# TensorE in program order: a delta rule and an attention woven between steps of twelve products

## The chip, the cores and the metric

The kernel runs on one core of one Trainium2 chip. The metric is the device time in microseconds of one execution; the time given for a kernel is the median of its runs. The profile and the trace are of one more execution, taken by the hardware profiler.

## The reference

One inference step of a two-layer decoder on 256 prompt tokens and 8 x 4 sample tokens (288 columns in all), model width 2048. Cut to what matters:

```python
for l in range(2):
    h = rmsnorm(x, norm_mix[l])
    if l == 0:   # gated delta rule, 12 heads of 128, chunks
        qkv, z, a, b, q_mem = split(h @ w_in)            # 2048 -> 4608 + 1536 + 24 + 512
        qkv = silu(causal_conv4(qkv)); q, k = l2norm(q), l2norm(k)
        beta, g = sigmoid(b), -exp(a_log) * softplus(a + dt_bias)
        # per chunk: solve (I + strict(k k^T * decay) * beta) [u, w] = [v beta, k beta gamma]
        # u -= w S; o = q_g S + (q k^T * decay) u; S = S * g_end + k_end^T u
        y_tok = rmsnorm(o) * silu(z)
    else:        # four causal pooling windows, a grouped projection
        y_tok, q_mem = pool_mixer(h)
    y_mem = cross_attn(q_mem, mem_k[l], mem_v[l])        # 4 heads, 256 memory tokens
    x = x + concat(y_tok, y_mem) @ w_out[l]
    x = x + (silu(rmsnorm(x) @ w_gate) * (rmsnorm(x) @ w_up)) @ w_down
y = rmsnorm(x)
```

Memory keys and values of the prompt are projected in the kernel (`mem_kv`); those of the eight samples are read from a cache (16 loads of 512 KB for each layer). States and caches are outputs too.

## The kernel before

Activations lie transposed, 128 features by 288 tokens to a tile. Every large product is computed from three products of rounded parts: a weight tile is split into `whi` (by ScalarE, L130) and `wlo` (by VectorE, L131), an activation into `xh` and `xl`, and L160, L161 and L162 issue `wh*xh`, `wh*xl` and `wl*xh`, 288 columns each. A weight chunk is one load of 512 KB (three buffers, tag `wraw`), and gives eight such products, 24 matmuls. `gemm_steps` is a generator over chunks: it yields once for a chunk. `mem_kv` does the same with 512 columns (L286 to L288). Products accumulate in four PSUM banks (`acc`); everything else that TensorE does writes one of four `aux` banks.

The order of the stages: `kq(0)` projects keys and queries of the first two heads while x is loaded; `x_norm` loads the rows of x (L248) for the norm's scale `rs0`; `alpha_beta` and `rates`, then `decays`, make the decay rates; then six units of two heads each. `Unit.keys` builds the triangular matrices and inverts them: squares and scales, `la` (L794, L800), then four levels of 32x32 blocks (L852 transposes on VectorE, L860 multiplies, ScalarE copies, L876 multiplies, VectorE merges at L885), then joins of blocks up to 128 and `wk`. `Unit.values` follows with the values, the states and the output; its last loads and stores are the sample states (L1011, L1104 to L1123). `gate` transposes the result and multiplies it into `y`. `drain` takes one piece of each of its generators in turn: a piece of `values` of one unit, one of `keys` of the next, one of `attention(0)`, one chunk of the projections for later units. After the sixth unit come the output projection `out_proj`, the feed-forward network (`ffn`, two thirds of all products), then the second layer: queries, `mem_kv(1)`, the pooling projections with `attention(1)` between them, `out_proj`, `ffn` and the final norm.

The code is a program in one order; a scheduler at compile time then lays out each engine's own queue: it takes instructions by priority (earlier in the program first, weights' splits raised by `high_priority`) when its own model of time says that they are ready. On the chip each engine, and SP's queue of loads, runs its list as laid out, and waits by semaphores. So in the kernel before a small matmul can stand anywhere in TensorE's queue, and a product of the next chunk can be put ahead of a part that the model thinks late.

`Norm.rstd` is the scale of a norm that the feed-forward network and the queries need: three column sums on TensorE (L210), a reciprocal square root of some twelve small VectorE operations (L105 to L111), three matmuls that spread it over the partitions (L235).

Of the kernel before, what the change touches and what calls it, by code (L numbers as in the profile page):

```python
# [16 lines left out]
P = 128  # L17
# [35 lines left out]
def VZ(n):  # L53
    return [24 + 2 * n, 25 + 2 * n] + ([36 + 2 * n, 37 + 2 * n] if n < 5 else [])
# [3 lines left out]
def body(ctx: ExitStack, tc: tile.TileContext, i: dict, o: dict):  # L58
# [13 lines left out]
    EV = 100  # L72

# [70 lines left out]
    def gemm_steps(chunk, ncols, kt, act, on_block, ks=2, order=None, bank=None, parts=1):  # L144
# [4 lines left out]
        for k0 in order:  # L149
            nk = min(ks, kt - k0)  # L150
            w = wchunk(chunk(k0 // ks), nk, ncols, parts=parts if k0 == 0 else 1)
            last = k0 == order[-1]
            kj = [(k, j) for k in range(nk) for j in range(nb)]
            for k, j in sorted(kj, key=lambda t: t[1]) if last else kj:
# [4 lines left out]
                en = last and k == nk - 1  # L159
                nc.tensor.matmul(pv, wh, xh, start=st, stop=False)  # L160
                nc.tensor.matmul(pv, wh, xl, start=False, stop=False)  # L161
                nc.tensor.matmul(pv, wl, xh, start=False, stop=en)  # L162
                if en:
                    on_block(j, pv)
            yield
# [14 lines left out]
    class Norm:  # L180
# [25 lines left out]
        def rstd(self):  # L206
            ps = aux()
            for t in range(3):
                rows = P if t < 2 else NS
                nc.tensor.matmul(  # L210
# [19 lines left out]
    def spread_psum(r):  # L230

        ps = aux()
        for t in range(3):
            rows = P if t < 2 else NS
            nc.tensor.matmul(  # L235
# [8 lines left out]
    def row_squares(src, rows, out):  # L244

        for h in range(2):
            t = wpool.tile([P, 1024], F32, name="rows", tag="wraw", bufs=3)[:rows]
            nc.sync.dma_start(t, src[:, h * 1024 : (h + 1) * 1024])  # L248
            nc.scalar.activation(t, t, AF.Square, accum_out=out[:rows, h : h + 1])

    def mem_norm():
        q = sp.tile([P, 2, 2], F32, name="mq", tag="mq", bufs=1)
        for t in range(2):
            row_squares(i["mr"][t * P : (t + 1) * P], P, q[:, t])
# [16 lines left out]
    def mem_kv(l, mem, part_tile, half, kt_, v_):  # L271
        mt = []
        pss = [[acc() for _ in range(2)] for _ in range(2)]
        for k0 in range(0, KT, 2):
            for k in (k0, k0 + 1):
                mt.append(split(mem(k), memw(l, k), hi=part_tile(), lo=part_tile()))
            for part in range(2):
                w = wchunk(i["wkv"][l, part, k0 // 2], 2, 512)
                for t in range(2):
                    for k in range(2):  # L280
# [5 lines left out]
                        nc.tensor.matmul(pv, xh, w[k][0], start=st, stop=False)  # L286
                        nc.tensor.matmul(pv, xl, w[k][0], start=False, stop=False)
                        nc.tensor.matmul(pv, xh, w[k][1], start=False, stop=en)  # L288
                yield
        for t in range(2):  # L290
# [11 lines left out]
            for h in range(NMH):  # L302
                nc.tensor.transpose(
# [8 lines left out]
    pad = cp.tile([P, 2, NMH, 2 * SHIFT + TS], F32, name="pad")  # L312
# [26 lines left out]
    rs0 = sp.tile([P, NT], F32, name="rs0", tag="rs0", bufs=1)  # L339
# [18 lines left out]
    def attention(l, ys, g2, s4, ahead):  # L358
        y = ys[NH:]
        for h in range(NMH):  # L360
            ps = aux()
            pv = ps.rearrange("p (t m) -> p t m", t=2)
            for t in range(2):
                nc.tensor.matmul(
# [13 lines left out]
            for t in range(2):  # L378
                nc.vector.tensor_scalar(e[:, t, :], e[:, t, :], sm[:, t : t + 1], None, op0=ALU.mult)
            pt = aux()  # L380
            ptv = pt.rearrange("p (m t) -> p m t", m=2)
            for m in range(2):
                for t in range(2):
                    nc.tensor.transpose(
# [3 lines left out]
            nc.vector.tensor_copy(pT, ptv)  # L388
            po = aux()
            for m in range(2):  # L390
                nc.tensor.matmul(
# [4 lines left out]
            yield  # L396
# [1175 lines left out]
```

## Time and profile before

| what | value |
|---|---|
| three runs | 2729.25, 2724.21, 2725.95 us; median 2725.95 |
| the profiled execution | 2727.26 us, of which the trace's span is 2725.5 us |
| TensorE, matmuls and weight loads | 2657.4 us and 2571.2 us busy, 21400 of each |
| VectorE, ScalarE, GpSimd | 1593.0, 1237.9 and 316.5 us busy |
| mean granted TensorE clock | 0.987 of full speed |
| moved by DMA | 455.86 MB, mean 167 GB/s |

How to read it: matmuls are pipelined, so the time of one is longer than its distance to the next, and a busy TensorE is not one at its peak. In the rows below PE is the matmuls' record and PEld that of the weight loads, of which each matmul has one. "Idle before" names what an engine waited for. The delta rule and the first attention run up to about 650 us, the first feed-forward network up to about 1590 us, the pooling layer with the second attention from 1600 to 1800 us, the second feed-forward network up to the end.

### The profile page before, as it was taken

Reading aid. Unit: us, or ns where it says so; the run is one execution under the profiler, and the core shown is the slowest. Engines: PE = TensorE matmul, PEld = TensorE weight load, DVE = VectorE, ACT = ScalarE, POOL = GpSimd, SP = SyncE. Lnnn points to the kernel's source line nnn. Section 1 sums busy time; section 2 is a strip of 40 time slices with the busy share of each in tenths; the row PEclk is TensorE's granted clock in tenths of the full one; section 3 lists DMA queues with packets and bytes.
Section 4 is the critical chain, followed back from the end, with each engine's and each line's share of the span. In section 5 each row is a group of like instructions: output and inputs, shape, how many; then the busy total and the mean of one; then the engine's idle time right before and its main releaser. Section 6 shows DMA issues by size and latency. Waiting matters only on the chain. (4 is left out here: it accounts for less than half of the span.)

```text
span 2725.5 us, 54445 instructions
## 1 busy us (share of the span) xinstructions
PE 2657.4 (98%) x21400; PEld 2571.2 (94%) x21400; DVE 1593.0 (58%) x3178; ACT 1237.9 (45%) x2407; POOL 316.5 (12%) x620
## 2 busy tenths in 40 slices
PE   7899999999999999999999999999999999999998
PEld 6888888788999999999999988899999999999997
DVE  5558776777655555445555566766555544555544
ACT  5454444444544444344444454455444433444443
POOL 0103221221101000000010111111001000001000
PEclk8999999999999999999999999999999999999998
DMA  7374345434545445455554575655455544545453
GB/s 255 122 233 134 102 151 171 143 118 169 164 164 169 167 166 168 165 169 165 170 166 167 166 248 160 216 174 162 164 170 164 169 167 166 167 166 170 164 170 128
DMA packets 133424, 455.86 MB, mean 167 GB/s; under 512 B 19440, under 2 KB 22000, under 8 KB 133168
## 3 DMA queue, kind: packets, MB, share of 16 engines
q1 hardware_dynamic: 133168, 452.38, 50.1%
q8 instruction: 168, 2.75, 0.4%
q14 instruction: 88, 0.72, 0.1%
HBM read 439.46 MB, written 12.86 MB: 166 GB/s over the span
## 5 line engine op out<-in xcount | busy, mean ns | idle before, releaser
L131 DVE TENSOR_TENSOR wlo<-wraw,whi 128x512 fp32r<-128x512 f32 (+1 forms) x1548 | 1066.6, 696 | 976.7 <-ACT whi L130 946.7
L130 ACT CAST whi<-wraw 128x512 fp32r<-128x512 f32 (+1 forms) x1548 | 939.7, 614 | 1214.2 <-PE acc L161 1128.4
L160 PE MATMUL acc<-a,whi 128*128 128x288 f32 x4864 | 1445.0, 297 | 19.0 <-ACT whi L130 19.0
L162 PE MATMUL acc<-a,wlo 128*128 128x288 f32 x4864 | 1443.8, 297 | 0.0
L161 PE MATMUL acc<-a,whi 128*128 128x288 f32 x4864 | 1443.4, 297 | 0.0
L160 PEld LDWEIGHTS acc<-a,whi 128*128 128x128 f32 x4864 | 918.6, 189 | 24.8 <-ACT whi L130 20.2
L162 PEld LDWEIGHTS acc<-a,wlo 128*128 128x128 f32 x4864 | 918.2, 189 | 5.6 <-issue 2.4
L161 PEld LDWEIGHTS acc<-a,whi 128*128 128x128 f32 x4864 | 918.9, 189 | 3.9 <-issue 1.4
L160 PE MATMUL acc<-b,whi 128*128 128x288 f32 x960 | 282.3, 294 | 0.0
L162 PE MATMUL acc<-b,wlo 128*128 128x288 f32 x960 | 282.3, 294 | 0.0
L161 PE MATMUL acc<-b,whi 128*128 128x288 f32 x960 | 282.3, 294 | 0.0
L1227 POOL TENSOR_TENSOR b<-b,rrow 128x288 f32<-128x288 f32 x88 | 89.4, 1034 | 1259.8 <-ACT b L1226 1259.8
L160 PEld LDWEIGHTS acc<-b,whi 128*128 128x128 f32 x960 | 180.1, 188 | 0.0
L162 PEld LDWEIGHTS acc<-b,wlo 128*128 128x128 f32 x960 | 180.1, 188 | 0.0
L161 PEld LDWEIGHTS acc<-b,whi 128*128 128x128 f32 x960 | 180.1, 188 | 0.0
L195 POOL TENSOR_TENSOR ssum<-ssum,sq 128x288 f32<-128x288 f32 x56 | 53.0, 947 | 427.6 <-ACT sq L194 425.6
L286 PE MATMUL acc<-whi,a 128*128 128x512 f32 x128 | 50.9, 406 | 5.1 <-ACT a L174 5.1
L288 PE MATMUL acc<-wlo,a 128*128 128x512 f32 x128 | 50.2, 393 | 0.0
L1225 DVE TENSOR_TENSOR b<-acc,rrow 128x288 f32<-128x288 f32 x88 | 40.1, 456 | 16.1 <-PE acc L162 16.1
L1226 ACT ACTIVATE b<-b 128x288 f32<-128x288 f32 x88 | 36.6, 439 | 26.1 <-DVE b L1225 25.8
L1231 DVE TENSOR_TENSOR b<-acc,b 128x288 f32<-128x288 f32 x88 | 39.9, 454 | 1.6
L690 DVE SCALAR_TENSOR_TENSOR ckq<-xp,cols,ckq 128x312 f32<-128x312 f32 x72 | 37.2, 547 | 0.7 <-ACT ckq L688 0.5
(378 smaller groups left out, 1607.0 us busy)
## 6 DMA issues: line engine op xcount, KB each, us to landing
wraw<-in_wgu_dram SPq DMA_DIRECT2D x352, 512.0 KB, 3.3
wraw<-in_wdn_dram SPq DMA_DIRECT2D x176, 512.0 KB, 3.2
wraw<-in_w_dram SPq DMA_DIRECT2D x103, 512.0 KB, 3.7
wraw<-in_wout_dram SPq DMA_DIRECT2D x64, 512.0 KB, 3.3
wraw<-in_wkv_dram SPq DMA_DIRECT2D x32, 512.0 KB, 4.2
wraw<-in_w1u_dram SPq DMA_DIRECT2D x32, 384.0 KB, 3.2
s<-in_dS_dram SPq DMA_DIRECT2D x12, 512.0 KB, 4.8
out_dram<-s SPq DMA_DIRECT2D x12, 512.0 KB, 3.8
```

Of the source, the lines that this page charges most:

```text
L130: nc.scalar.copy(hi[:, :n], src)
L131: nc.vector.tensor_tensor(lo[:, :n], src, hi[:, :n].bitcast(F32), op=ALU.subtract)
L160: nc.tensor.matmul(pv, wh, xh, start=st, stop=False)
L161: nc.tensor.matmul(pv, wh, xl, start=False, stop=False)
L162: nc.tensor.matmul(pv, wl, xh, start=False, stop=en)
L195: nc.gpsimd.tensor_tensor(self.sum, self.sum, q, op=ALU.add)
L286: nc.tensor.matmul(pv, xh, w[k][0], start=st, stop=False)
L288: nc.tensor.matmul(pv, xh, w[k][1], start=False, stop=en)
L690: nc.vector.scalar_tensor_tensor(c[:, :312], xp[:, q : q + 312], convw(q, f), c[:, :312], op0=ALU.mult, op1=ALU.add,)
L1225: nc.vector.tensor_tensor(t, ps, rs, op=ALU.mult)
L1227: nc.gpsimd.tensor_tensor(t, t, rs, op=ALU.mult)
L1231: nc.vector.tensor_tensor(t, ps, t, op=ALU.mult)
```

## The change

All matmuls and transposes now go through `mm` and `tr`, which give each one an ordering edge to the one before it: TensorE's queue is the program's order, and the scheduler still orders the other engines. A chunk yields twice, after each twelve matmuls (a step; nine in the pooling projections, three in their grouped ones). `weave` counts steps: before each it runs those parts of its lanes that are due, and a lane's `yield n` says that its next part comes n steps later. `keys` becomes 16 parts (at steps 0, 4, 9, 10, 12, 13, 15, 16, 18, 19, 21, 22, 24, 25, 26 and 28 of a unit's weave), `values` 8 parts (from step 4: 4, 6, 8, 10, 13, 16, 18, 20, the last with what was `gate`), an attention head three. A unit's weave has 32 steps of products for units 0 to 2, 24 for units 3 and 4, and for unit 5 ten steps of the output projection, which now starts there. Rows of x and of the memory are loaded into the tag `ck` (three buffers) where they took weight buffers; `rates` and `decays` move behind the first projection, as a lane. `rstd` stays a plain call. Some copies and scalings of `keys` and `attention` go from VectorE to ScalarE, two predicated copies become one, the padded queries of the attention's value part get a buffer of their own for each of two samples, and the last state product of `values` moves up and holds an `aux` bank of its own (`pe`) beside `po` and `pz`.

```diff
+    def in_order(ins):
+
+        if last[0] is not None:
+            tc.add_manual_dep(
+                ins.ins, last[0].name,
+                mybir.DependencyInfo(
+                    mybir.DependencyClass.NoSync, mybir.DependencyReason.DATA
+                ),
+                reason="order",
+            )
+        last[0] = ins.ins
+        return ins
+
+    def mm(*args, **kw):
+        return in_order(nc.tensor.matmul(*args, **kw))
...
+            if last_:
+                kj.sort(key=lambda t: t[1])
+            n = 0
+            for k, j in kj:
...
+                n += 1
+                if n % max(1, len(kj) // 2) == 0:
+                    yield
...
-    def row_squares(src, rows, out):
+    def row_squares(src, rows, out, tile_):
 
         for h in range(2):
-            t = wpool.tile([P, 1024], F32, name="rows", tag="wraw", bufs=3)[:rows]
+            t = tile_([P, 1024])[:rows]
...
-    def mem_norm():
+    def mem_norm(tile_):
...
+                    yield
...
-    pad = cp.tile([P, 2, NMH, 2 * SHIFT + TS], F32, name="pad")
+    pad = cp.tile([P, 2, 2, NMH, 2 * SHIFT + TS], F32, name="pad")
...
-    rs0 = sp.tile([P, NT], F32, name="rs0", tag="rs0", bufs=1)
+    rs0 = sp.tile([P, NT], F32, name="rs0", tag="rrow", bufs=1)
...
-    def x_norm():
+    def x_rows(tile_):
         q = sp.tile([P, 3, 2], F32, name="xq", tag="xq", bufs=1)
         for t in range(3):
             rows = P if t < 2 else NS
-            row_squares(i["xr"][t * P : t * P + rows], rows, q[:, t])
+            row_squares(i["xr"][t * P : t * P + rows], rows, q[:, t], tile_)
+        return q
+
+    def x_norm(q):
...
-                nc.vector.tensor_scalar(e[:, t, :], e[:, t, :], sm[:, t : t + 1], None, op0=ALU.mult)
+                nc.scalar.activation(e[:, t, :], e[:, t, :], AF.Copy, scale=sm[:, t : t + 1])
+            yield 4
...
-            nc.vector.tensor_copy(pT, ptv)
+            nc.scalar.copy(pT, ptv)
+            yield 2
...
-                nc.gpsimd.tensor_copy(pad[:, :, :, SHIFT : SHIFT + TS], pT[:, :, :, b, :])
+                nc.gpsimd.tensor_copy(pad[:, b % 2, :, :, SHIFT : SHIFT + TS], pT[:, :, :, b, :])
...
+    class Lane:
+
+
+        def __init__(self, gen, wait=0):
+            self.gen, self.at, self.live = gen, wait, True
+
+        def go(self, now):
+            while self.live and self.at <= now:
+                n = next(self.gen, self)
+                if n is self:
+                    self.live = False
+                else:
+                    self.at = now + max(1, n or 1)
+
+    def weave(filler, lanes, side=None):
+
+        now, more = 0, True
+        if side:
+            side.at = 0
+        while more or any(t.live for t in lanes):
+            for t in lanes + ([side] if side else []):
+                t.go(now)
+            if more:
+                more = next(filler, lanes) is not lanes
+            now += 1
...
+    def out_proj(l, order, after, ys=None):
+
+        ys = {} if ys is None else ys
+
+        def load(g, c):
+            p = order.index(c)
+            for k in (2 * q + n for q in order[p : p + 2] for n in range(2)):
+                if k not in ys:
+                    ys[k] = split(y[k])
+            return i["wout"][l, g, c]
...
-        gp = tiles("u", 8)
+        gp = tiles("u", 4)
+        gp4 = tiles("la", 2)
...
-            rates(pab)
...
+            return pab
...
-                dt = decay(h0)
-                pk, pz, pq = aux(), aux(), aux()
+                pk, pz = aux(), aux()
+                pq = pz[:, 320:326]
...
-                nc.vector.tensor_copy(krf.rearrange("p c d -> p (c d)"), pk)
-                nc.vector.tensor_copy(kr_s.rearrange("p h d -> p (h d)"), pz[:NS3, : 2 * P])
+                nc.scalar.copy(krf.rearrange("p c d -> p (c d)"), pk)
+                nc.scalar.copy(kr_s.rearrange("p h d -> p (h d)"), pz[:NS3, : 2 * P])
...
-                yield
+                yield 4
 
                 stt = nc.vector.scalar_tensor_tensor
-                la = {}
+                la = gp4([P, 2, 2, 2, P])
+                la = {t: la[:, t] for t in range(2)} | {"all": la}
...
-                    for t in range(2):
-                        cp_(
-                            uc[bl(q), 2 * t : 2 * t + 2, :], mask(1, bl(q), 2),
-                            la[t][bl(q), :, 0, bl(q)],
-                        )
+                    cp_(
+                        uc[bl(q), 0:4, :].rearrange("p (t h) c -> p t h c", t=2),
+                        lev[1][bl(q)].unsqueeze(1).unsqueeze(1).broadcast_to([32, 2, 2, 32]),
+                        la["all"][bl(q), :, :, 0, bl(q)],
+                    )
...
+                yield 5
...
+                    yield 1
...
+                    yield 2
...
-                cc(U[lo, :, hi], pZ[lo])
+                nc.scalar.copy(U[lo, :, hi], pZ[lo])
...
+                pe = aux()
+                for hh in range(2):
+                    mm(H(pe, hh), kend[:, 1, hh, :], u[1][:, hh, :], start=True, stop=True)
...
-        x_block(0)
-        next(first)
-        for n in range(1, 6):
+        for n in range(6):
             x_block(n)
-            next(first)
+            steps(first, 2)
         load_constants()
         nc.sync.dma_start(cst[:, :, 3:27], i["convT"])
         nc.sync.dma_start(alog, i["a_log"][0].partition_broadcast(P))
         nc.sync.dma_start(dtb, i["dt_bias"][0].partition_broadcast(P))
-        x_norm()
-        steps(first, 1)
-        alpha_beta()
-        steps(first, 1)
-        decays()
+        xq = x_rows(ck)
+        ab = alpha_beta()
+        steps(first, 2)
+        x_norm(xq)
         drain(first)
 
         def mem_part():
-            mem_norm()
+            mem_norm(ck)
             yield from mem_kv(0, mem_blocks(ck), lambda: at(F32R)[:, :NM], ga, KT_, V_)
 
-        drain(units[0].keys(), chain(vz(0), project_q(), mem_part(), kq(1)))
+        z = lambda n: project(96 + 4 * n, [44 + 2 * n, 45 + 2 * n])
+
+        def rates_keys():
+            rates(ab)
+            yield 4
+            decays()
+            yield 2
+            yield from units[0].keys()
+
+        weave(chain(vz(0), project_q(), mem_part(), kq(1)), [Lane(rates_keys(), 1)])
+        att = Lane(attention(0, y, ga, ck, 2))
+        out = out_proj(0, (0, 1, 2, 3, 4, 6, 7, 5), lambda k: n1.add(k, x[k], ffnw(0, k)))
+        n1 = Norm()
+        x = []
         for n in range(6):
+            lanes = [Lane(units[n].values(), 0 if n == 5 else 4)]
             if n < 5:
-                gem = [vz(n + 1)] + ([kq(n + 2)] if n < 4 else [])
-                side = take(att, 20 if n == 4 else 4) if n >= 1 else iter(())
-                drain(units[n].values(), units[n + 1].keys(), side, chain(*gem))
-            else:
-                conv_state()
-                drain(units[n].values(), project(100, [46, 47]))
-            units[n].gate()
+                lanes.insert(0, Lane(units[n + 1].keys()))
+            if n == 4:
+                lanes.append(att)
+            filler = (
+                chain(kq(n + 2), vz(n + 1)) if n < 4 else chain(vz(5), z(0), z(1)) if n == 4
+                else take(out, 10)
+            )
+            weave(filler, lanes, att if 1 <= n < 4 else None)
+        conv_state()
...
-                    steps(gate, 6)
+                    steps(gate, 12)
...
-        n1 = Norm()
-        drain(out_proj(0, (0, 1, 2, 3, 4, 6, 7, 5), lambda k: n1.add(k, x[k], ffnw(0, k))))
+        drain(out)
...
-        drain(
+        weave(
             chain(
                 project_u(3), project_u(2), group(3, acc), project_u(1), group(2, acc),
                 project_u(0),
             ),
-            slowly(att),
+            [Lane(attention(1, y, ga, s4, 3), 3)],
```

## Rows read from the trace of the kernel before

**Rows 1.** The page, busy time of TensorE.

```profile
PE 2657.4 (98%) x21400; PEld 2571.2 (94%) x21400; DVE 1593.0 (58%) x3178; ACT 1237.9 (45%) x2407; POOL 316.5 (12%) x620
```

**Rows 2.** Windows: busy us of PE, PEld, DVE, ACT, POOL, clock; sum over 200:650.

```profile
250.00:300.00 50.00, 49.48 (x558) 45.87 (x558) 34.99 (x89) 25.40 (x53) 9.66 (x32) 1.00 0.55 169
...
sum 450.00, PE 427.42 PEld 380.12 DVE 338.87 ACT 203.55 POOL 122.16; mean PE 47.49 PEld 42.24 DVE 37.65 ACT 22.62 POOL 13.57
```

**Rows 3.** The same view, other stretches: feed-forward network, pooling layer.

```profile
1000.00:1200.00 200.00, 200.00 (x1521) 200.00 (x1521) 98.69 (x155) 80.75 (x135) 4.10 (x4) 1.00 0.50 167
1600.00:1700.00 100.00, 98.42 (x580) 86.70 (x579) 68.12 (x146) 51.40 (x110) 12.53 (x30) 1.00 0.56 179
1700.00:1800.00 100.00, 96.93 (x814) 90.07 (x814) 72.54 (x174) 49.00 (x106) 17.47 (x51) 0.98 0.63 207
```

**Rows 4.** Timeline of TensorE, two levels of the inversion: start, us, line.

```profile
105.96 0.29 PE L162 MATMUL acc<-a,wlo 128*128 128x288 f32 x1
106.18 0.45 PE L860 MATMUL aux<-h,u 32*32 32x32 f32 x32
106.56 0.40 PE L160 MATMUL acc<-a,whi 128*128 128x288 f32 x1
106.80 0.30 PE L161 MATMUL acc<-a,whi 128*128 128x288 f32 x1
...
107.15 0.45 PE L876 MATMUL aux<-uc,h 32*32 32x32 f32 x32
...
108.65 0.45 PE L860 MATMUL aux<-h,u 32*32 32x32 f32 x32
```

**Rows 5.** Timeline of TensorE: one unit's first key transposes, its first level.

```profile
393.35 0.49 PE L751 MATMUL aux<-ident,ckq 128*128 128x128 f32 x3
...
421.87 0.42 PE L860 MATMUL aux<-h,u 32*32 32x32 f32 x29 [1.45 <-ACT v L1077]
```

**Rows 6.** Timeline of TensorE, the start.

```profile
41.23 0.61 PE L160 MATMUL acc<-a,whi 128*128 128x288 f32 x1 [12.40 <-ACT whi L130]
...
49.46 4.66 PE L611 MATMUL aux<-a,wraw 128*32 128x288 f32 x64
```

**Rows 7.** Timeline of SP's queue, the start.

```profile
24.43 9.43 SPq L248 DMA_DIRECT2D rows<-in_xr_dram  x6
36.84 0.35 SPq L120 DMA_DIRECT2D wraw<-in_w_dram  x1
```

**Rows 8.** Timeline of TensorE: `rates`, `decays`.

```profile
54.82 0.53 PE L532 MATMUL aux<-masks,g 128*128 128x32 f32 x4
...
73.81 0.67 PE L576 MATMUL aux<-gg,masks 128*128 128x24 f32 x4 [1.07 <-DVE gg L558]
...
75.46 0.46 PE L576 MATMUL aux<-gx,ones 32*128 32x96 f32 x2
...
78.54 0.60 PE L594 MATMUL aux<-gam,masks 32*128 32x6 f32 x4
```

**Rows 9.** Timeline of TensorE, the first products of `mem_kv(0)`.

```profile
137.36 1.22 PE L286 MATMUL acc<-whi,a 128*128 128x512 f32 x2 [3.97 <-ACT a L174]
```

**Rows 10.** Timeline of TensorE: a norm's scale, before the first feed-forward network.

```profile
759.00 0.51 PE L210 MATMUL aux<-ones,ssum 128*128 128x1 f32 x4
759.45 0.40 PE L160 MATMUL acc<-a,whi 128*128 128x288 f32 x1
...
763.07 1.04 PE L235 MATMUL aux<-ident,c3y 128*128 128x128 f32 x6
```

**Rows 11.** Timeline of TensorE, the last norm's scale at the end.

```profile
2712.72 1.75 PE L235 MATMUL aux<-ident,c3y 128*128 128x128 f32 x6 [2.50 <-DVE c3y L111]
```

**Rows 12.** Line L457 in 1600:1800: what TensorE sat idle for, us, times.

```profile
  POOL pad L454: 6.8, 7
```

**Rows 13.** VectorE's groups by form in 200:650: count, busy us, mean ns.

```profile
L131 DVE TENSOR_TENSOR wlo<-wraw,whi 128x512 fp32r<-128x512 f32 x159 | 110.5, 706 | 58.5 <-ACT whi L130 52.5 <-PE aux L876 1.9 <-ACT u L915 1.3
...
L841 DVE COPY_PREDICATED uc<-levels,u 32x64 f32<-32x64 uint8 x40 | 14.0, 386 | 0.3
```

More of the change, by code (lines that the diff above doesn't have):

```diff
@@ L158, in gemm_steps @@
                 st = k0 == order[0] and k == 0
[L159 to L162, printed above, removed]
+                en = last_ and k == nk - 1
+                mm(pv, wh, xh, start=st, stop=False)
+                mm(pv, wh, xl, start=False, stop=False)
+                mm(pv, wl, xh, start=False, stop=en)
                 if en:
                     on_block(j, pv)
-            yield
+                n += 1
+                if n % max(1, len(kj) // 2) == 0:
+                    yield
     def split(src, scale=None, hi=None, lo=None):
@@ L476, in drain, with steps @@
     def drain(*gens):
-        live = list(gens)
-        while live:
-            for g in list(live):
-                if next(g, live) is live:
-                    live.remove(g)
+        for g in gens:
+            for _ in g:
+                pass
+    def steps(g, n):
+        for _ in range(n):
+            next(g, None)
     def take(g, n):
@@ L486, in take, with on @@
             yield
-    def steps(g, n):
-        for _ in range(n):
-            next(g, None)
+    class Lane:
[26 more added lines that the diff above has]
+            return i["wout"][l, g, c]
+        for g in range(4):
+            def on(j, ps):
+                k = 4 * g + j
+                nc.vector.tensor_tensor(x[k], x[k], ps, op=ALU.add)
+                after(k)
+            yield from gemm_steps(
+                lambda c: load(g, c), 512, KT, lambda k: ys[k], on,
+                order=[2 * c for c in order],
+            )
     y = [None] * 16
@@ L760, in keys @@
                     )
-                for hh in range(2):
-                    for t in range(3):
-                        rows = P if t < 2 else NS
-                        n = t * 2 + hh
-                        nc.tensor.matmul(
-                            pq[:rows, n : n + 1], q2[hh][:, t * P : t * P + rows], ones[:, 0:1],
-                            start=True, stop=True,
-                        )
                 ts = nc.vector.tensor_scalar
@@ L797, in keys @@
                         )
+                    for hh in range(2):
+                        ts_ = slice(t * P, (t + 1) * P)
                         n = t * 2 + hh
@@ L811, in keys @@
                     )
+                for hh in range(2):
                     for m, sc in ((0, nrb), (1, rk)):
@@ L1283, in body @@
         queries = gemm_steps(lambda c: i["w1q"][c], 512, KT, n2.act, on_q)
-        steps(queries, 6)
+        steps(queries, 12)
         rs1 = n2.rstd()
@@ L1366, in body @@
         )
-        steps(out, 5)
+        steps(out, 8)
         drain(group(1, aux))
         drain(group(0, aux))
-        steps(out, 4)
+        steps(out, 8)
         nc.sync.dma_start(o["pool"], st)
```

197 lines of the change are left out of this document (94 added, 103 removed).

## The prediction

> **What bounds the kernel now.** I read the page first, then windows by stage, then the timelines of the places that stood out. TensorE is the bound from end to end: its matmuls' record is busy 98% of the span [rows 1]. How much of that is product? In the feed-forward network 1521 matmuls take 200 us, 131.5 ns each, and both records are full [rows 3]; a step of twelve is 1.58 us. Nothing can be won there. In the delta rule the two records part: from 200 to 650 us the matmuls' record misses 22.6 of 450 us, the weight loads' 69.9 [rows 2]. Every matmul has a weight load, so a stretch in which the loads pause is one in which the array isn't fed, though a long matmul record still covers it. I take the 69.9 us as the room there. VectorE has 338.9 us of work in the same 450, ScalarE 203.6 [rows 2]: neither is full, but VectorE is near enough to hold up a chain. Other room: 12.4 us of waiting for weights at the start [rows 6], 4.0 before the memory projection [rows 9], 23.2 us of paused weight loads in the pooling layer [rows 3].
>
> [...] By the one record here the core could give 22.6 us at most, by the other 69.9; the full stretch of the feed-forward network, where the two agree, speaks for the second.
>
> **The change, part by part.** Sums are against the profiled execution, 2727.3 us (2725.5 of span and 1.8 around it), 1.3 above the median of the runs shown.
>
> *The weave, 200 to 650 us.* It adds no product. Each part that stands between products costs a turn: before the 32x32 group the distance is 0.22 us in place of 0.13, after it 0.24 in place of 0.13, so 0.20 for the two [rows 4]. With 24 parts in each of six units and 22 of the attention, 166 parts, this is 33 us that no order removes. Do the parts come in time? In a level the second group follows the first after 0.97 us and the next level after 1.50 [rows 4]; the weave gives them one and two steps, 1.6 and 3.2 us, so there is cover as long as VectorE's queue is not over 1.6 us late. The long chain is the one from the first key transposes to the first level: 28.5 us in the unit shown, with 1.45 of waiting at its end [rows 5]. The weave gives it nine steps, 14.2 us, and whatever parts stand between. It is also made shorter: half as many predicated copies, which were 40 of 386 ns [rows 13], and copies that leave VectorE; ScalarE has 246 us free for them [rows 2]. What stands against it: VectorE's splits of weights alone are 110.5 us [rows 13], and a late one now stops TensorE, where before another instruction could stand there. Units 3 and 4 have 24 steps for 28 due, and unit 5 has ten for some eighteen, so the last parts there have no cover. I cannot price every part; I take the best stretch of the kernel before, 4.13 us of pause in 50 with units running [rows 2], as what the whole core becomes: nine times this is 37.2, a gain of 32.7 us. Bounds: nothing, and 69.9 - 33.2 = 36.7.
>
> [...]
>
> *The start.* SP issues the six row loads over 9.43 us, each waiting for a weight buffer, and the next weights go out only at 36.84 [rows 7]; TensorE waits 12.4 us [rows 6]. In buffers of their own three rows go at once, and weights needn't wait behind the others if the compiler's list puts them ahead; the rows still end when they end, the spread of the norm now stands before the last chunk, and behind it everything on TensorE. So what can move into the hole is the seventh chunk (24 x 0.1315 = 3.2) and the 64 small products of `alpha_beta`, 4.66 [rows 6]: 7.8 us. Bounds: 0 (SP's list keeps the rows first, with wab's load and the weights queued behind them) and 12.4.
>
> *Rates and decays.* Before, 19.0 us pass between the products of `rates` and those of `decays`, and TensorE idles 1.07 of them [rows 8], because products of the next projection stand between. Now four steps, 6.3 us, stand there, and what is late stops all of TensorE. The chain is some forty small VectorE operations among the convolutions of four heads. Bounds: 19.0 - 6.3 = 12.7 if nothing speeds it up; the nearest row for a bare chain is a norm's root, a third of it, 3.6 us from 759.45 to 763.07 [rows 10], so 10.9 - 6.3 = 4.6. Inside `decays` the last products wait for an exponential, 2.6 us from 75.92 to 78.54 [rows 8], with no step between. I take 9 + 3 = 12 lost; bounds 4.6 + 2.6 = 7.2 and 12.7 + 2.6 = 15.3.
>
> *Memory projection.* The squares of the memory's rows leave the weight buffers as well: the 4.0 us [rows 9] go (bound 0).
>
> *Norm scales.* Here strict order costs for certain. Before, 28 products fill the 3.6 us between the column sums and the spread [rows 10]; `rstd` has no step inside, so TensorE now stands still there, at both feed-forward networks and at the queries. At the end of the kernel, where nothing fills it, the same wait shows 2.50 us idle [rows 11]. I take 3.5 each, 10.5 us lost; bounds 7.5, three times the end's wait, and 12, three times the nearest longer pause [rows 9].
>
> *Pooling layer.* Two copies of the padded queries end the 6.8 us that the attention waits for GpSimd [rows 12]. The parts come closer together, so the cache loads may be late in their place. I take 6.8; bounds 0, and the 23.2 us [rows 3] less 0.20 for each of the 22 parts, 18.8.
>
> The rest costs nothing while it is covered: `rs0` in the buffer of the later norm row (that row is written after the last use), half the `u` buffers with `la` in its own two, the output projection's splits, made two chunks ahead of their products by ScalarE and VectorE.
>
> Sum: 2727.3 - 32.7 - 7.8 - 4.0 - 6.8 + 12 + 10.5 = 2698.5, or 2697 against the median.
>
> **The rivals.** *Everything covered*: all terms at their better bounds, 2727.3 - 36.7 - 12.4 - 4.0 - 18.8 + 7.2 + 7.5 = 2670. For it: the levels' cover is twice their need [rows 4]. Against it: the units without steps at their end. *Core unmoved*: VectorE and the four `aux` banks (`po`, `pz`, `pe` held at once leave one) set the pace, TensorE's holes only move: 2698.5 + 32.7 = 2731.2, or 2730 against the median. For it: VectorE has on average 37.65 us of work in 50 [rows 2], and less time for it where TensorE gains. *Slower*: in strict order the parts come late by VectorE's queue. Where 166 parts wait on average 0.22 us beyond their turn, the core's 69.9 us are back; at 0.35 us it is 91 us, and the time 2698.5 + 91.3 - 37.2 = 2752.6, about 2751. For it: the 28.5 us chain against nine steps [rows 5]. Against it: a late part gives all later ones more time.
>
> **How the numbers follow.** Two runs of this kernel can differ by about 0.2%, 5.5 us, so faster is under 2720.5 and slower over 2731.4. Forecast 0.52, with 2682 to 2720 as its own range; everything covered 0.18; core unmoved 0.11, which falls within; slower 0.19. The range leaves out half of the slower case and a little of the covered one: 2660 to 2738.
>
> **What would show it.** Right: the weight loads' record in the delta rule pauses about 4 us in 50 or less, and the stage ends some 30 us earlier; three holes of 3 to 4 us between a norm's column sums and its spread; a hole of about 9 us before the products of `decays`; no wait for GpSimd's padded queries. Wrong: waits at the first level of each unit, at splits (`wlo`) or for `aux` banks that sum to 70 us; a granted clock below 0.9 in the core; or holes at the norms that aren't there because products still stand in them.

## The result: 2.8% slower, where 1% faster was forecast

The changed kernel takes 2804.66 us (median of 4 runs, 2800.91 to 2808.93), the kernel before 2727.6 beside it: a ratio of 1.0281, 95% interval 1.0256 to 1.0305. The prediction was 2697 with a range of 2660 to 2738, so the sign is wrong and the time lies 67 us outside.

The head of the page of the changed kernel (span; then busy time and share of each engine):

```profile
span 2799.0 us, 54381 instructions
PE 2668.8 (95%) x21400; PEld 2587.5 (92%) x21400; DVE 1567.5 (56%) x3112; ACT 1259.6 (45%) x2451; POOL 320.7 (11%) x620
```

TensorE's share fell from 98% [rows 1] to 95%. Where the 73.5 us of span went is read from the start times of four instructions in both traces: the first product of the first memory projection, the first column sum of the first feed-forward norm, the first product of the second memory projection, the first column sum of the third norm. Between them lie five stages, in us:

```
                                start   delta   ffn 0   pooling  rest
kernel before                   137.4   621.5   846.2   284.3    836.1
changed kernel                  137.9   665.3   855.9   299.8    840.1
changed, order left free        128.4   621.4   846.2   284.0    835.9
changed, two orders             132.8   618.0   846.2   291.4    835.9
changed, parts first            135.6   642.0   855.7   288.2    841.5
changed, steps in the norms     136.6   666.2   848.7   299.7    838.7
changed, free, rows early       119.9   621.7   846.3   284.4    835.9
kernel before, order fixed      167.4   806.3   854.6   319.2    840.2
```

(The lower six are the experiments below. In the one with steps in the norms the first and the third norm's column sums stand 24 products, or 3.2 us, earlier in TensorE's order, so in its row the delta rule and the pooling layer end that much sooner, and the stage behind each starts that much sooner.) Of the first two lines the difference is +0.5, +43.8, +9.7, +15.5 and +4.0. The delta rule lost most. Windows of the changed kernel (busy us of PE, PEld, DVE, ACT, POOL with the number of instructions; then the granted clock, DMA share, GB/s):

```profile
200.00:650.00 450.00, 396.34 (x4250) 355.95 (x4250) 288.48 (x811) 196.54 (x500) 117.69 (x276) 0.94 0.39 126
...
265.00:273.00 8.00, 0.69 (x33) 0.33 (x20) 8.00 (x28) 4.61 (x11) 4.14 (x12) 0.82 0.26 81
...
555.00:565.00 10.00, 2.62 (x42) 2.04 (x41) 10.00 (x34) 5.23 (x11) 4.98 (x13) 0.77 0.26 90
```

Over the 450 us the weight loads pause 94.0 us, where they paused 69.9 [rows 2], and VectorE is *less* busy than before, 288 us for 339, in part because these 450 us hold less of the work. On the mean VectorE is far from full. The two short windows tell what the mean hides: for 8 us VectorE works without a break and TensorE does almost nothing. The waits of TensorE in the changed kernel (whose line waited for which releaser: us in total, times, longest):

```profile
PE aux L90 <- DVE uc L975: 14.8, 2, 7.4
PE aux L90 <- DVE c3y L132: 11.3, 4, 2.9
PE aux L93 <- DVE la L890: 10.5, 6, 3.5
PE aux L90 <- DMA wraw<-in_wab_dram: 9.4, 1, 9.4
PE aux L90 <- DVE v L1182: 7.4, 1, 7.4
PE acc L90 <- ACT whi L151: 6.6, 1, 6.6
PE aux L93 <- ACT ag L409: 6.5, 2, 5.5
PE aux L90 <- DVE gg L640: 5.5, 1, 5.5
PE aux L93 <- DVE ag L474: 5.0, 1, 5.0
```

Most of these are small products or transposes (`aux`), and most releasers are VectorE's. Now the longest of them, first on TensorE, then on VectorE (start, duration, line, out<-in, count, idle time before and its releaser):

```profile
264.81 0.45 PE L90 MATMUL aux<-uc,h 32*32 32x32 f32 x32
265.19 0.50 PE L90 MATMUL aux<-ue,kE 96*128 96x512 f32 x1
273.06 0.77 PE L90 MATMUL aux<-ue,kE 96*128 96x512 f32 x1 [7.38 <-DVE uc L975]
```

```profile
265.09 1.29 DVE L152 TENSOR_TENSOR wlo<-wraw,whi 128x512 fp32r<-128x512 f32 x2
266.31 1.00 DVE L126 TENSOR_SCALAR c6y<-ov 128x6 int32<-128x6 int32 x1
267.22 0.53 DVE L776 SCALAR_TENSOR_TENSOR ckq<-xp,cols,ckq 128x312 f32<-128x312 f32 x1
267.68 0.16 DVE L127 TENSOR_SCALAR c6y<-c6y 128x6 int32<-128x6 int32 x1
267.75 0.53 DVE L776 SCALAR_TENSOR_TENSOR ckq<-xp,cols,ckq 128x312 f32<-128x312 f32 x1
268.20 0.16 DVE L130 TENSOR_TENSOR c6t<-c6y 128x6 f32<-128x6 f32 x1
...
272.55 0.16 DVE L1181 TENSOR_TENSOR c6y<-c6y,scal 128x6 f32<-128x6 f32 x1
272.63 0.28 DVE L975 COPY_PREDICATED uc<-levels,aux 128x128 f32<-128x128 uint8 x1
272.83 0.41 DVE L1182 TENSOR_TENSOR v<-aux,c6y 128x256 f32<-128x256 f32 x1
```

The second group of products of a level ends at 265.26; the merge that reads it (L975, 0.28 us) runs at 272.63, after splits of weights, nine taps of convolutions (L776, 0.53 us each) and a root of eleven small operations (L126 to L132). The merge is what releases the second product of `ue` and `kE` (most likely because that product needs the `aux` bank that the merge frees), and in the fixed order all products of the projections stand behind it. The same happens in other units: TensorE waits 7.42 and 7.38 us ahead of a product of `ue` and `kE` that starts at 471.35 and at 563.77.

In the rows above the merge could have run for 7.4 us and stands behind the 24 instructions that VectorE starts in that time, and on TensorE no product passes the one that waits: from 265.69 to 273.06 none runs there.

### The profile page after: what moved, and what is told of

Read it like the earlier page. It is cut to its first block, busy times and chain, and to the rows that moved or that the text cites. A ratio compares the mean times of both kernels' runs of the same rounds, so it can differ in the third digit from the quotient of the medians.

```text
span 2799.0 us, 54381 instructions
## 1 busy us (share of the span) xinstructions
PE 2668.8 (95%) x21400; PEld 2587.5 (92%) x21400; DVE 1567.5 (56%) x3112; ACT 1259.6 (45%) x2451; POOL 320.7 (11%) x620
## 4 chain that ended last, share of the span: by engine, by line
PE 91%; DVE 5%; DMA 1%; ACT 1%; issue 1%; SPq 0%; POOL 0%; DVEq 0%; ACTq 0%
PE acc L90 84%; PE aux L90 6%; DVE wlo L152 1%; PE aux L93 1%; DVE ckq L776 1%; ACT whi L151 0%; DMA ck<-in_xr_dram 0%; SPq L1251 0%; DVE la L890 0%; DMA ck<-in_cv_dram 0%; DMA wraw<-in_w_dram 0%; DVE xp L753 0%; DMA ck<-in_ckT_dram 0%; DVE cv L776 0%; POOL pad L454 0%
## 5 line engine op out<-in xcount | busy, mean ns | idle before, releaser
L90 PE MATMUL acc<-a,whi 128*128 128x288 f32 x9728 | 1967.4, 298 | 12.2 <-ACT whi L151 6.6
L90 PEld LDWEIGHTS acc<-a,whi 128*128 128x128 f32 x9728 | 1574.4, 190 | 23.0 <-issue 10.1
L90 PE MATMUL acc<-b,whi 128*128 128x288 f32 x1920 | 379.7, 294 | 0.0
L90 PEld LDWEIGHTS acc<-b,whi 128*128 128x128 f32 x1920 | 306.5, 188 | 0.0
L90 PE MATMUL acc<-whi,a 128*128 128x512 f32 x192 | 65.6, 395 | 1.1 <-ACT a L200 1.1
L90 PEld LDWEIGHTS acc<-whi,a 128*128 128x128 f32 x192 | 36.0, 188 | 9.8 <-ACT a L200 1.6
L776 DVE SCALAR_TENSOR_TENSOR ckq<-xp,cols,ckq 128x312 f32<-128x312 f32 x72 | 37.1, 533 | 0.5 <-ACT ckq L774 0.2
L1205 POOL TENSOR_TENSOR ue<-uH,masks 96x512 fp32r<-96x512 f32 x24 | 31.0, 1310 | 51.5 <-DVE uH L1140 30.7
L90 PE MATMUL aux<-ue,kE 96*128 96x512 f32 x24 | 11.5, 527 | 25.9 <-DVE uc L975 14.8
L201 DVE SCALAR_TENSOR_TENSOR a<-x,cols,a 128x288 fp32r<-128x288 f32 x48 | 34.6, 721 | 2.4 <-ACT a L200 0.8
```

The source lines that it names most:

```text
L90: return in_order(nc.tensor.matmul(*args, **kw))
L201: nc.vector.scalar_tensor_tensor(lo, src, scale, hi.bitcast(F32), op0=ALU.mult, op1=ALU.subtract)
L776: nc.vector.scalar_tensor_tensor(c[:, :312], xp[:, q : q + 312], convw(q, f), c[:, :312], op0=ALU.mult, op1=ALU.add,)
L1205: gt(ue, uH[:, hh, :].bitcast(F32).unsqueeze(1).broadcast_to([NS3, 4, P]), bmask[:, 4 * c : 4 * c + 4].unsqueeze(2).broadcast_to([NS3, 4, P]),
```

## The experiments

**Theory A:** a part that comes late stops all of TensorE, since products can't pass it in the fixed order; it is late because it stands in VectorE's queue behind convolutions. **Rival B:** the four `aux` banks, three held by `po`, `pz`, `pe`, set the pace. **Rival C:** not the order but the weave itself (places and number of the parts) costs.

**Order left free.**

```
-        if last[0] is not None:
+        if False:
             tc.add_manual_dep(
                 ins.ins, last[0].name,
...
```

> The changed kernel with the dependence between successive matmuls left out, all else as changed (parts, steps, buffers). Theory A, a late part stops all of TensorE because of the fixed order: other products go past a late part again, the norms' scales get cover back (three holes of 3.6 us) and the delta rule gives back most of the 44 us that it grew by (first norm sums from 803 to about 765 us): 2740 to 2760. Rival C, the weave itself (fewer, other places for the parts) costs the time whatever the order: 2785 to 2805, only the three holes go.

Measured 2718.69 us, ratio to the kernel before 0.9961 (0.9948 to 0.9974). So the fixed order costs 2804.66 - 2718.69 = 86 us, more than expected, and without it the change is a gain of 9 us or so. In the table every stage becomes shorter, by 9.5, 43.9, 9.7, 15.8 and 4.2: the losses go, and the start gains 9 us. Rival C falls. But the delta rule takes 621.4 us, against 621.5 before: the weave wins nothing there even in the free order. One thing moves along: without the edges the compiler lays out VectorE's queue anew as well (some 350 of its 3112 instructions stand more than five places from where they stood), so the 86 us are the price of the order with what follows from it in the other queues.

**Three taps of four left out, in the changed kernel and in the kernel before.**

```
-                for q in range(1, 4):
+                for q in range(1, 1):
                     nc.vector.scalar_tensor_tensor(
                         c[:, :312], xp[:, q : q + 312], convw(q, f), c[:, :312],
...
```

> The changed kernel with three of the four taps of the convolution left out (108 VectorE operations of 0.53 us, 57 us of VectorE; the output is another one). Theory A, the parts come late because VectorE's queue is full where a projection's four blocks end: the delta rule's end comes 30 to 45 us earlier, 2760 to 2775. Rival B, the four aux banks (three held by the output's norm) set the pace whatever VectorE's queue holds: less than 10 us, 2795 to 2805.

> The kernel before with the same three taps left out, so the other half of the comparison. Theory A: in the free order products fill the time in which VectorE is late, so little comes back, 2 to 12 us: 2715 to 2725. If VectorE's queue paces the kernel before just as much, it gains as many us as the changed one, 2680 to 2695.

Measured 2772.91 and 2722.82: with the fixed order 57 us less work on VectorE are worth 31.8 us, without it 5.7 (2728.54 for the kernel before, beside it). The banks are the same as without the edit, so the banks alone can't be the cause of these 32. The group of the products of `ue` and `kE` from 200 to 700 us, of the changed kernel and then with one tap (busy us, mean ns, idle before and its releasers):

```profile
L90 PE MATMUL aux<-ue,kE 96*128 96x512 f32 x24 | 11.5, 527 | 25.9 <-DVE uc L975 14.8 <-DVE v L1182 7.4 <-DVE c6y L132 2.0
```

```profile
L90 PE MATMUL aux<-ue,kE 96*128 96x512 f32 x24 | 10.5, 466 | 6.5 <-DVE c6y L132 2.0 <-DVE v L1182 1.9 <-DVE ov L1179 1.1
```

The wait named `uc` is gone: the bank passed on that VectorE was late. Whether one bank more would have taken the wait away as well was not tried, so B stands as a part of the cause that is not excluded.

**The state's products five steps later.**

```
-                yield 3
+                yield 8
                 for hh in range(2):
                     s = s0[hh]
```

> The changed kernel with eight steps in place of three between the output's norm and the state's products ue x kE, whose matmuls waited 25.2 us in 13 places between 250 and 640 us. Theory A: VectorE has worked off its queue by then, so most of the 25 us goes: 2780 to 2792. Rival, the wait moves to the next part (the gates or the next unit's levels): 2797 to 2808.

Measured 2795.35, between the two expectations. Here are the same group, and the row that now leads the waits from 200 to 700 us:

```profile
L90 PE MATMUL aux<-ue,kE 96*128 96x512 f32 x24 | 8.4, 423 | 1.8 <-DVE ov L1179 1.1 <-DVE s L1216 0.6
```

```profile
PE aux L90 <- DVE h L941: 16.7, 4, 6.7
```

24 us of waiting were taken away and 9.3 came back: the transposes that open a level (L941, 2.6 us of waiting in the changed kernel) are now what TensorE waits for, behind the same burst on VectorE. More cover for one part uncovers the next.

**The parts ahead in the queues,** in the fixed and in the free order.

```
-                n = next(self.gen, self)
+                with tc.high_priority(offset=300):
+                    n = next(self.gen, self)
```

> The changed kernel, order of TensorE fixed, in which the operations of the woven parts stand ahead in the queues of VectorE and ScalarE (their priority in the compiler's list is raised by 300 places, so they go before convolutions and splits that came earlier). No work is left out. Theory A in its narrow form (a part is late because it stands behind convolutions in VectorE's queue, not because VectorE has too much work): as much comes back as without the three taps, 31.8 us, or more: 2750 to 2778. Rival, the sum of VectorE's and the chain's work sets the pace, and a splitting of weights that is now late takes the place of the late part: 2795 to 2825.

> The same priority without the fixed order of TensorE. Theory A: where products can pass a late part there is little to win: 2710 to 2722 beside 2718.7 for the free order alone. If the queue order costs in the free kernel too, 2695 to 2708; if the priority makes TensorE take small parts where they wait, over 2725.

With the fixed order 2766.63: 38 us come back with no work left out, by the places of the parts in the other engines' queues alone (delta rule 665.3 to 642.0, pooling layer 299.8 to 288.2). What takes their place leads the waits now, the emptying of the projections' accumulators:

```profile
PE acc L90 <- DVE xp L757: 13.8, 4, 4.1
```

In the free order the same priority costs 16 us, 2734.65, a time of the expectation's third case. That TensorE took small parts where they wait, as that case says, was not shown; what leads TensorE's waits on VectorE there is again the emptying of the accumulators (`xp`), 8.4 us, which does not stand among the waits of the free order alone.

**Steps inside the norms.**

```
-                    steps(gate, 12)
-                    rs = nrm.rstd()
+                    steps(gate, 10)
+                    r = nrm.rstd_sums()
+                    steps(gate, 4)
+                    rs = spread(r)
```

(and the same for the queries)

> The changed kernel with the column sums of the three norms two steps earlier and their spread four steps (6.3 us) after the sums, so that products of the gates and of the queries stand between. Theory A: the three holes of 3.6 us go, 10.8 us, and up to 5 more that the clock at half speed behind each of them cost: 2788 to 2795. Rival, the hole moves to the first gate that needs the spread row: 2800 to 2808.

Measured 2791.64, 13.0 us less. TensorE at the first norm, the changed kernel and then this one:

```profile
803.23 0.65 PE L90 MATMUL aux<-ones,ssum 128*128 128x1 f32 x6
806.83 1.01 PE L90 MATMUL aux<-ident,c3y 128*128 128x128 f32 x3 [2.95 <-DVE c3y L132]
```

```profile
802.81 0.65 PE L90 MATMUL aux<-ones,ssum 128*128 128x1 f32 x6
...
809.81 0.27 PE L90 MATMUL aux<-ident,c3y 128*128 128x128 f32 x1
```

**The kernel before with the fixed order and nothing else.**

```
+    def omm(*args, **kw):
+        return in_order(nc.tensor.matmul(*args, **kw))
...
-                nc.tensor.matmul(pv, wh, xh, start=st, stop=False)
+                omm(pv, wh, xh, start=st, stop=False)
```

(`in_order` is that of the changed kernel; so for every matmul, and by `otr` for every transpose)

> The kernel before with nothing but TensorE's fixed order added (each part one step of 24 products as before). Theory A: the fixed order costs here at least as much as the 86 us that it costs in the changed kernel, and the weave of finer steps is what lessens it: 2815 to 2900. If the order costs only with the new weave (shorter steps, other places), 2727 to 2760.

Measured 2991.14, far over the expectation: there the fixed order costs 262 us (2729.34 for the kernel before, beside it). Its waits are led by VectorE's names, its clock fell to 0.82 in the same window:

```profile
200.00:650.00 450.00, 355.29 (x3090) 311.59 (x3089) 245.53 (x647) 151.05 (x368) 82.34 (x214) 0.82 0.33 106
```

```profile
PE aux L89 <- DVE u L820: 26.7, 12, 5.7
PE aux L89 <- DVE c3y L131: 25.5, 5, 14.2
PE aux L92 <- DVE ag L399: 24.9, 7, 5.1
```

So under a fixed order the rest of the change (the finer weave with the moved copies, buffers and rates, not taken apart) is worth 2991.14 - 2804.66 = 186 us; it just doesn't make up for the order.

**Can the fixed order be mended?** The norms' steps, the parts 200 places ahead, the accumulators' emptying 400 places ahead (`EV = 400`).

> The changed kernel, order fixed, with the parts 200 places ahead in the list, the multiplications that empty the projections' accumulators 400 places ahead of all (in the variant with the parts first TensorE waited 13.8 us for these), and the norms' steps. Theory A, the waits are VectorE's queue order and can be taken off one by one: 2766.6 - 13 for the norms - 10 for the accumulators = 2735 to 2750. Rival, VectorE's total work is the limit under a fixed order, so each wait taken away comes back elsewhere: 2750 to 2770.

Measured 2767.53: the rival. The wait for `xp` went from 13.8 to 2.8 us, as meant, and others came up:

```profile
PE aux L93 <- DVE la L891: 10.7, 5, 3.5
...
PE aux L90 <- DVE c6y L132: 6.3, 3, 2.6
...
PE acc L90 <- DVE xp L757: 2.8, 1, 2.8
```

Three things differ from the run with the parts first, so this shows only that these mends don't add up, not which of them lost.

**Two orders in place of one.**

```
-    def in_order(ins):
+    def in_order(ins, chain="parts"):
...
+    def gm(*args, **kw):
+        return in_order(nc.tensor.matmul(*args, **kw), "products")
```

(`gm` in `gemm_steps` and `mem_kv`, `mm` and `tr` elsewhere, one `last` for each chain)

> The changed kernel with two orders in place of one: the products of the projections and of the memory in their order among themselves, the small products and transposes of the parts in theirs, and nothing between the two, so that a product can pass a late part. Theory A: what costs is that products stand behind late parts, so nearly all of the 86 us comes back: 2717 to 2732. Rival, the order among the parts themselves (a unit's values behind the next unit's keys) costs as well: 2745 to 2785.

Measured 2723.99, ratio 0.9981 (0.9970 to 0.9992): 81 of the 86 us are the products' standing behind parts. The two orders cost the other 5 or so, and beside the free order the table has a loss in the pooling layer (291.4 for 284.0) and at the start (132.8 for 128.4); the delta rule is 3.4 us shorter, 618.0 for 621.4. Windows of this kernel:

```profile
200.00:650.00 450.00, 426.93 (x4594) 380.39 (x4593) 315.21 (x884) 216.78 (x555) 129.65 (x284) 0.99 0.44 140
...
436.00:444.00 8.00, 5.86 (x72) 5.41 (x71) 8.00 (x26) 5.67 (x11) 3.83 (x9) 1.00 0.34 118
```

Read the last line beside 265 to 273 of the changed kernel: VectorE is full for 8 us in both, TensorE works 5.86 us here and 0.69 there. It is the same place of a unit, as TensorE's own rows show:

```profile
436.60 0.45 PE L90 MATMUL aux<-uc,h 32*32 32x32 f32 x32
436.98 0.50 PE L90 MATMUL aux<-ue,kE 96*128 96x512 f32 x1
437.32 0.43 PE L93 MATMUL acc<-a,whi 128*128 128x288 f32 x2
...
446.97 0.47 PE L90 MATMUL aux<-ue,kE 96*128 96x512 f32 x1
```

The second product of `ue` and `kE` comes 9.99 us after the first, later than the 7.87 us of the changed kernel, but products of the projections (L93) run in between, with one wait of 2.14 us. The bursts on VectorE are still there; TensorE has something else to do.

**What wins the 9 us in free order?** The row buffers alone in the kernel before; and the free kernel with the rows back in the weights' buffers.

```
-            t = wpool.tile([P, 1024], F32, name="rows", tag="wraw", bufs=3)[:rows]
+            t = tile_([P, 1024])[:rows]
```

(`tile_` is `ck`; in the second run the other way round)

> The kernel before with one part of the change alone: the rows of x and of the memory go through the three ck buffers, not through the weights'. If this alone is what the free-order variant of the changed kernel wins over the kernel before (its weight loads pause 6.5 us less between 14 and 140 us, and nothing less from 210 to 700): 2716 to 2722. Rival, the new order of the first projections wins it and the buffers are indifferent: 2725 to 2731.

> The changed kernel in free order with the rows of x and of the memory back in the weights' buffers. In the kernel before the row buffers alone gave nothing (2727.7), so if parts add up this stays at 2716 to 2721 and the weave with the new first stage has won the 10 us; rival, the row buffers win only together with the new order of the first stage (the spread ahead of the last chunk): 2724 to 2730.

Measured 2727.71 (ratio 0.9995, 0.9985 to 1.0004) and 2717.40. The row buffers win nothing in either kernel. In the kernel before they bring the first memory product 4.5 us forward, from 137.4 to 132.9, but the delta rule then takes 626.7 us in place of 621.5: time won at the start need not last. The 9 us of the free order do last. They lie ahead of the first memory product, and with the row buffers excluded the new order of the first projections, rates and keys is what remains. Which part of that order wins them was not taken apart.

**The rows of x early,** in the free order.

```
-        load_constants()
+        nc.sync.dma_start(ident, i["ident"])
+        nc.sync.dma_start(masks, i["masks"])
+        nc.sync.dma_start(cols[:, 32:], i["cols"][:, 32:])
+        ab = alpha_beta()
+        steps(first, 2)
+        xq = x_rows(ck)
+        x_norm(xq)
         nc.sync.dma_start(cst[:, :, 3:27], i["convT"])
+        drain(first)
         nc.sync.dma_start(alog, i["a_log"][0].partition_broadcast(P))
         nc.sync.dma_start(dtb, i["dt_bias"][0].partition_broadcast(P))
-        xq = x_rows(ck)
-        ab = alpha_beta()
-        steps(first, 2)
-        x_norm(xq)
-        drain(first)
+        nc.sync.dma_start(levels, i["levels"])
```

> The changed kernel in free order, with the load of the small projection's weights, one more chunk and the rows of x issued ahead of the constants that are needed later (they stood 23.96 us into the span, behind a broadcast load that SP issued for 5.60 us). The rows then come about 8 us earlier: the 8.5 us wait for that load goes and the spread of the norm is done by 40 us in place of 47.5. Theory, the start is the one place where cover is missing in free order: 2708 to 2714. Rival, the transfers compete with the first chunks and splits of weights and give it back: 2716 to 2722.

Measured 2711.49, ratio 0.9940 (0.9928 to 0.9953): the best version found, 0.6% under the kernel before and 7.2 us under the free order alone. The wait for `wab`'s load, 8.5 us in the free kernel, is gone from TensorE's list, and the start stage is 8.5 us shorter (119.9 for 128.4).

## Why the prediction was wrong, by its own steps

**The weave in the delta rule, -32.7 forecast, +43.8 measured: the step that failed.** It asked whether the parts come in time, answered that there is cover "as long as VectorE's queue is not over 1.6 us late", and then took the best stretch of the kernel before for the whole. The condition was the right one and was never tested: VectorE's mean of 37.65 us in 50 says nothing of bursts. When a projection's last chunk is through, its four blocks end close together and each puts three taps of 0.53 us into the queue with the scaling; parts behind them came up to 7.4 us late. The kernel before has such bursts too, and windows as short as they are show them; but other products filled TensorE's time there, as in the run with two orders. One of them in the kernel before (VectorE, the third, is busy for all of 8 us, TensorE for 7.59):

```profile
604.00:612.00 8.00, 7.59 (x111) 6.82 (x109) 8.00 (x28) 3.67 (x10) 1.04 (x1) 1.00 0.54 192
```

A stretch of a kernel in free order was used as the measure of a kernel in fixed order. And with the order free the weave is worth 0.1 us in this stage, with two orders 3.5, so the 32.7 weren't there to be had by these steps at all: in the free order the weight loads pause 70.0 us from 200 to 650 us, as before the change. What makes them pause there was not taken apart.

**The rival on the other side was the right mechanism, too small.** It set 0.35 us beyond its turn for each of 166 parts. The stage came out 43.8 + 32.7 = 76.5 us over the forecast, which itself held 37.2 us of pause, together 113.7, part of which is a lower clock (0.94 from 200 to 650 us, 0.97 before). By the rival's own division, less the 33.2 us that the parts' turns cost, this is 80.5 / 166 = 0.48 us. The nine largest rows of TensorE's waits from 200 to 700 us hold 52 us, single waits of up to 7.4 us that no mean shows. Its chance of 0.19 was too low: what spoke for it (one queue, a long chain, nine steps) was a cause, and what spoke against it (a late part gives later ones time) only a hope.

**The start, rates and decays, memory: -7.8, +12 and -4.0 forecast, +0.2 in sum; +0.5 measured.** The sum is right in part by luck. The order's price fits: 9.5 us (137.9 for 128.4) for 12. The wait of 4.0 us before the memory's products [rows 9] did go. But the reason of the gain was wrong: the row buffers are worth nothing in the end, and the hole at the start only shrank from 12.4 [rows 6] to 9.4. TensorE's waits in the changed kernel from 14 to 80 us:

```profile
37.23 6.21 PE L90 MATMUL aux<-a,wraw 128*32 128x288 f32 x64 [9.40 <-DMA wraw<-in_wab_dram]
54.85 0.57 PE L90 MATMUL acc<-a,whi 128*128 128x288 f32 x2 [2.73 <-DVE xp L756]
...
69.48 1.05 PE L90 MATMUL aux<-gg,masks 128*128 128x24 f32 x4 [5.49 <-DVE gg L640]
72.68 1.02 PE L90 MATMUL aux<-gam,masks 32*128 32x6 f32 x4 [0.61 <-ACT gam L671]
```

What was to stop TensorE did so: 5.49 us at the rates where 9 were taken, and 0.61 where 3 were.

**The norms' scales, +10.5 forecast.** Right: holes of 3.6 us from sums to spread at all three places; steps inside them gave 13.0 us back, 2.2 more than the holes, which I put down to the clock (below).

**The pooling layer, -6.8 forecast, +15.5 measured.** The 6.8 us [rows 12] were read too large: that view adds the idle time of the matmuls and of the weight loads. The matmuls alone waited 2.8 us for the copies of the value part's padded queries, in the kernel before from 1600 to 1800 us:

```profile
PE aux L457 <- POOL pad L454: 2.8, 2, 2.6
```

This wait did go. The changed kernel's row for a padded query is a copy of the scores' part (L454 there; the value part's copy is L488 and is in no row), from 1600 to 1820 us:

```profile
PE aux L90 <- POOL pad L454: 0.3, 1, 0.3
```

What took its place is the same mechanism as in the delta rule. The two rows on `ag` in the list of waits at the head, 6.5 and 5.0 us, lie in the same stretch: the softmax's chains in the attention now hold up the products. The prediction looked for late cache loads there and not for this. With the order free the stage is as long as before, 284.0 us for 284.3, so the wait for the padded queries wasn't on the path either.

**What was to show the forecast wrong** named waits at the first level and at splits (`wlo`) and a clock under 0.9. No wait for `wlo` stands among TensorE's, and the clock was 0.94. The long waits came at the state's products and at transposes, behind VectorE's merges and scalings (L975 14.8 us, L890 10.5); most likely they are waits for `aux` banks, as that list had it, but they are far from 70 us. The sign of a right forecast failed clearly: the weight loads pause 94.0 us in 450, 10.4 in 50, where 4 were asked.

## What to carry to other kernels

Fixing the order of TensorE's instructions made a producer's *latest* delivery count here in place of its mean (waits of up to 7.4 us for VectorE, which is busy 288 us of 450): look at the other engines' queues in windows as short as the cover that a part has, not in windows of 50 us. Where products are at hand that depend on nothing late, leave them free to pass, or fix two orders, one for the products and one for the parts: here this took away 81 of 86 us. A stretch of a kernel whose scheduler fills holes shows what filling hides; it is no forecast for the kernel that may not fill them.

## What the runs showed of the hardware

Holes in the changed kernel cost more than their length. After the wait of 7.38 us that ends at 273.06, and after the 2.95 us at the first norm, TensorE's granted clock is 0.50, and products start 0.24 us apart (the twelve from 273.63 to 276.51, the fifteen from 809.19 to 812.79), where the full stretch of the kernel before has 0.13 [rows 3]. Windows of the changed kernel, granted clock third from the end:

```profile
273.00:276.00 3.00, 2.94 (x11) 2.88 (x12) 3.00 (x7) 0.60 (x2) 1.55 (x5) 0.50 0.00 0
...
807.00:810.00 3.00, 3.00 (x12) 2.71 (x13) 0.46 (x1) 0.00 (x0) 0.00 (x0) 0.50 0.15 60
```

The first feed-forward stage, which holds the first norm and the queries' norm, is 9.7 us longer with two holes of 3.6; the other 2.5 us I put down to products at this clock. The kernel with two orders, where TensorE's longest wait from 200 to 700 us is 2.1, shows a granted clock of 0.99 from 200 to 650 us; the changed kernel, with waits of up to 7.4, shows 0.94.

The issue of one and the same load took very different times on SP's queue. The broadcast load of `alog` took 6.89 us to issue in the changed kernel, behind five loads of constants, and 0.42 us in the version with the rows early. The expectation above took its 5.60 us in the free order for the load's own price; the 0.42 speaks against that. In the changed kernel `alog` stands right behind the load of `convT`; in the version with the rows early a load of weights stands there, and that one took 4.77 us. What holds an issue up at this place was not looked into. SP's rows of `alog` in the one and the other:

```profile
16.35 6.89 SPq L1251 DMA_DIRECT2D alog<-in_a_log_dram  x1
```

```profile
35.83 0.42 SPq L1258 DMA_DIRECT2D alog<-in_a_log_dram  x1
```
